# Split first weight loads, regrouped statistics and key rope sums in a two-layer trunk kernel

## The chip, the cores and the metric

The kernel runs on one core of one Trainium2 chip. The metric is the device time of one execution in microseconds (us); several executions are timed and their median is given. A profile of one execution shows each instruction of the five engines: TensorE (PE in the profile, its weight loads PEld), VectorE (DVE), ScalarE (ACT), GpSimd (POOL) and SyncE (SP), which here issues most DMA transfers.

## The reference

Two layers work on 528 tokens (16 meta tokens and 512 of the sequence) with 1024 channels in float32. Per layer:

```python
h = rmsnorm(x)
u_pool, z_pool, c_q, c_kv, k_rope, z_mla, g_pool, g_mla = split(h @ w_in)
y_pool = (pool_mix(u_pool) * silu(z_pool)) @ pool_w_up      # causal means over 2, 4, 8, 16 tokens
y_mla  = (mla(c_q, c_kv, k_rope) * silu(z_mla)) @ mla_w_up  # latent attention, 8 heads
x = x + (sigmoid(g_pool) * y_pool + sigmoid(g_mla) * y_mla) @ w_out
```

In `mla`, `c_q` (768 wide) and `c_kv` (256 wide) are RMS-normalised over their own width and expanded to queries, keys and values. A key head is 64 channels from `c_kv` and 32 channels of `k_rope`, which all heads share. Keys and queries are RMS-normalised per head (96 channels), the 32 channels get a rotary embedding, and attention is causal.

## The kernel before, in words

**Layout.** Channels lie on the 128 partitions, tokens along the free dimension. An activation tile is 128 channels by 528 tokens, and a matmul takes half of them, 264 (`HALF`). The first norm is not applied ahead of the products: they use x times the gain, and the token's factor `inv` is multiplied in where a product leaves PSUM.

**Products in three parts.** Weights and activations are split into a high and a low part, each of a type that TensorE multiplies faster than float32. ScalarE makes the high part, VectorE the low part by a subtraction. `mm3` (L184 to L186) is the three matmuls high·high, low·high and high·low. `split_h` (L336, L338) splits an input tile into `hh` and `hl`; `wload` (L179, L180) splits a weight chunk of 128 × 512 into `whi` and `wlo`.

**One stream of products.** `plan` lists all GEMMs in order: ckv0, ckv1, cq0 to cq4, then u0, k0, u1, kr, k1, u2, k2, u3, k3, the values v, and so on. `stream` goes through their weight chunks, with loads three to four ahead: `fetch` (L114) is a DMA on SP's queue into one of three `raw` buffers. `step` emits the next few matmuls of the stream; `upto(name)` emits until that GEMM is done, and `fill_now(ns)` emits matmuls for about so much time. Everything else is written between these calls, so it stands between matmuls of the stream in the program. A scheduler then orders the instructions on each engine; `behind(a, b)` forbids it to put a ahead of b. PSUM has four banks "mm", three "S" and one "o".

**Start.** ScalarE's queue loads the first 512 columns (four blocks of 128, one for each of the first four input tiles) of ckv0's weights (L121). SP's queue loads the gains `gn` (L122), input tile 0 (L123), the same columns of ckv1's weights, input tile 1, then the other input tiles (`other_loads`). TensorE multiplies ones (L136) meanwhile.

**Norm sums.** `norm_sums` adds squares over channels with a matmul by ones (L389). In layer 0 the sums over x come from ScalarE, which squares and adds rows of x (`row_sums`, L363), while matmuls of the stream are emitted; the sums over `c_kv` come from the squares that ScalarE makes of the product (L447). The sums go through DRAM (`nsr`), VectorE computes inverse roots, these go to DRAM (`ndr`), and two DMAs broadcast them to all partitions (`inv`, `cinv`; L427). `RET` is the time that is filled with products meanwhile.

**Key rope part.** `kr_body` (L455) has 32 columns of weights only, so four groups of 32 columns of the array work side by side on four input tiles, in float32; ScalarE copies the result and VectorE adds the four groups (L468, three adds for each half of the tokens). Later (`rest`, after `LAG`) it is multiplied by `inv`, copied to a second place by POOL, squared, scaled and rotated (`rope`).

**Statistics.** `stat` collects squared tiles, and `stat_go` (L496) sums them per head with a matmul whose weights are 8 columns wide. Each of the two token halves has two column groups, so four run side by side. It is called twice a layer, with 5 members (keys, `k_sums`) and with 7 (queries). `k_factors` reads the keys' sums back from DRAM (`ka`, L518), computes inverse roots and spreads them.

Of the kernel before, what the change touches and what calls it, by code (L numbers as in the profile page):

```python
# [9 lines left out]
F32 = mybir.dt.float32  # L10
# [8 lines left out]
P = 128  # L19
# [52 lines left out]
def trunk(ctx, tc, xT, xrow, mrow, pos, win, wkr, wqb, wkb, wvb, wgr, wpu, wmu, wout, gains, const, yT):  # L72
# [49 lines left out]
    first = sp.dma_start(gn, gains)  # L122
# [36 lines left out]
    vt = cp.tile([P, 4, H, P], F32R, name="vt")  # L159

    class Gemm:
        def __init__(self, name, src, width, evac=None, xs=None, segs=None, body=None, gain=None):
            self.name, self.src, self.width, self.alloc = name, src, width, mmt
            self.evac, self.xs, self.segs, self.body, self.gain = evac, xs, segs, body, gain
            self.spare = False

    loads = [0]

    def wload(src, n, gain, spare):
# [3 lines left out]
        if gain is not None:  # L173
            v = raw[:, :n].rearrange("p (k m) -> p k m", k=8)
            gp.tensor_mul(v, v, gain.unsqueeze(2).to_broadcast([P, 8, n // 8]))
            return raw, None
        hi = pool.tile([P, W if pool is tp else 512], F32R, tag=th, name=nm("whi"), bufs=nb)
        lo = pool.tile([P, W if pool is tp else 512], F32R, tag=tl, name=nm("wlo"), bufs=nb)
        act.activation(hi[:, :n], raw[:, :n], AF.Copy)  # L179
# [12 lines left out]
    def stream():  # L192
        flat = [(g_, c) for g_ in plan for c in range(0, g_.width, 512)]
        flat[1], flat[2] = flat[2], flat[1]

        def load(i):
            g_, c = flat[i]
            n = min(512, g_.width - c)
            return wload(g_.src[:, c:c + n], n, g_.gain, g_.spare)

        ahead = []
        for i in range(4):
            ahead.append(load(i))
            yield 0.0
        for i, (g_, c) in enumerate(flat):
            w = ahead.pop(0)
            if i >= 3 and i + 1 < len(flat):
                ahead.append(load(i + 1))
            final = c + 512 >= g_.width
            if g_.body is not None:  # L210
                yield from g_.body(c // 512, w)
# [101 lines left out]
    class Layer:  # L313
# [34 lines left out]

        def row_sums(self):
            sx = sm.tile([P, 2, 5], F32, tag="sx", name=nm("sx"))  # L350
            tags = ("q4", "q5", "q6", "q7", "kn0", "kn1", "kn2", "kn3", "kp")
            rows = []
            for i in range(2 * len(tags) + 4):
                step()
                if i % 2 == 0 and len(rows) < len(tags):
                    k = len(rows)
                    r, src = (P, xrow[:, k]) if k < 8 else (2 * NM, mrow)
                    rows.append(slot(tags[k])[0:r, 0:512])
                    behind(sp.dma_start(rows[k], src), newest[0])
                if i % 2 == 1 and i >= 5:  # L360
                    k = (i - 5) // 2
                    t = rows[k]
                    made = act.activation(t, t, AF.Square, accum_out=sx[0:t.shape[0], k % 2, k // 2:k // 2 + 1])  # L363
                    behind(made, newest[0])
                yield
            raw = nsr[0]
            sp.dma_start(raw[0:2, NM:T].rearrange("h (p i) -> p h i", i=4), sx[:, :, 0:4])
            sp.dma_start(raw[0:2, 0:NM].rearrange("h m -> m h"), sx[0:2 * NM, 0, 4:5])

        def norm_sums(self):  # L370
# [14 lines left out]
            for k in range(0, len(runs), 2):  # L385
                for s, (a, b) in enumerate(FULL):
                    for ps, t, m, start, stop in runs[k:k + 2]:
# [34 lines left out]
            fill_now(RET / 2)  # L422
            if self.l == 0:
                tables()
            fill_now(RET / 2)
            for i, d in enumerate((self.inv, self.cinv)):
                behind(sp.dma_start(d[:, 0:T], norms[i:i + 1, :].partition_broadcast(P)), newest[0])  # L427
            self.st = [sct(), sct()]
# [18 lines left out]
                self.csq_last = act.activation(self.csq[m][:, a:b], ps, AF.Square)  # L447
            return ev

        def kr_body(self, _, w):  # L450
            for a, b in FULL:
                ps = mmt()
                for k in range(8):
                    g = 32 * (k % 4)
                    pe.matmul(ps[g:g + 32, :b - a], w[0][:, 32 * k:32 * k + 32], self.xt[k][:, a:b],  # L455
                              start=k < 4, stop=k >= 4, tile_position=(0, g))
                self.ev_kr(ps[:, :b - a], a, b)
                yield 9 * (b - a) / 2.4

        def ev_kr(self, ps, a, b):  # L460
            n = b - a
            if a == 0:
                self.kraw = slot("kn3")
                self.kp = slot("kp")
            t = tmp()
            act.activation(t[:, :n], ps, AF.Copy)
            for g in (32, 64, 96):
                dve.tensor_add(t[0:32, :n], ps[g:g + 32, :], t[0:32, :n])  # L468

            def rest():  # L470
                dve.tensor_mul(t[:, :n], t[:, :n], self.inv[:, a:b])
                gp.tensor_copy(t[64:96, :n], t[0:32, :n])
                q = sqt()
                made = act.activation(q[:, :n], t[:, :n], AF.Square)
                self.stat(q[:, :n], a, b, C_KPE, made)
                kr = self.kraw[:, a:b]
                act.activation(kr, t[:, :n], AF.Copy, scale=self.g(G_KR))
                self.rope(self.kp[:, a:b], kr, a, b)
# [9 lines left out]
        def stat_go(self, members):  # L488
# [3 lines left out]
            for k, (s, a, b, q, c, made) in enumerate(batch):  # L492
                n = count[s]
                count[s] += 1
                g = 32 * s + 64 * (n % 2)
                mm = pe.matmul(self.st[s][g:g + H, a:b], cst[:, c:c + H], q, start=n < 2, stop=n >= members - 2,  # L496
                               tile_position=(0, g))
                if k < len(batch) - 1:
                    behind(mm, batch[-1][5])

        def stat_rows(self, x0):
# [450 lines left out]
        def register(self, nxt):  # L952
# [65 lines left out]
        def go(self, nxt):  # L1018
            l = self.l
            up = lambda name: upto((l, name))  # L1020
            if l == 0:
                for k in range(8):
                    if k in (0, 1, 3, 5):
# [133 lines left out]
```

## Time and profile before

| | us |
|---|---|
| median of 3 runs | 781.39 (781.0 to 783.37) |
| the profiled execution | 781.23 |
| its span, first to last instruction | 779.4 |
| TensorE busy | 773.5 (99% of the span) |
| VectorE, ScalarE, GpSimd busy | 537.7, 414.7, 206.8 |

A line of a timeline gives the start in us from the span's start, the duration, engine, line of the kernel, operation, output and inputs, shape and count; in brackets stands how long the engine was idle ahead of it and who ended that. A line of a grouped view gives the count, busy time in us and the mean of one in ns, and after a bar the idle time ahead. A line of a table by stretches gives the stretch, its length, the busy time of PE, PEld, DVE, ACT and POOL with counts, the granted clock, the busy share of the DMA engines and what they moved in GB/s. Matmuls are pipelined: the distance between starts tells what one costs.

### The profile page before, as it was taken

Reading aid. Unit: us, or ns where it says so; the run is one execution under the profiler, and the core shown is the slowest. Engines: PE = TensorE matmul, PEld = TensorE weight load, DVE = VectorE, ACT = ScalarE, POOL = GpSimd, SP = SyncE. Lnnn points to the kernel's source line nnn. Section 1 sums busy time; section 2 is a strip of 40 time slices with the busy share of each in tenths; the row PEclk is TensorE's granted clock in tenths of the full one; section 3 lists DMA queues with packets and bytes.
Section 4 is the critical chain, followed back from the end, with each engine's and each line's share of the span. In section 5 each row is a group of like instructions: output and inputs, shape, how many; then the busy total and the mean of one; then the engine's idle time right before and its main releaser. Section 6 shows DMA issues by size and latency. Waiting matters only on the chain.

```text
span 779.4 us, 14500 instructions
## 1 busy us (share of the span) xinstructions
PE 773.5 (99%) x5235; PEld 702.8 (90%) x5235; DVE 537.7 (69%) x1155; ACT 414.7 (53%) x930; POOL 206.8 (27%) x265
## 2 busy tenths in 40 slices
PE   8999999999999999999999999999999999999998
PEld 8999899999999999999998898887788888888887
DVE  5588687357788977685465577774477888755932
ACT  6755655545565665643354355455445666654420
POOL 1034504012334242053120235130132433420500
PEclk9999999999999999999999999999999999999999
DMA  8533233433322212234643322434242332222372
GB/s 281 163 112 89 83 123 99 116 87 101 92 88 86 82 55 81 80 97 147 186 135 97 103 82 90 132 88 142 69 129 89 96 86 81 66 81 68 105 240 88
DMA packets 54931, 84.04 MB, mean 108 GB/s; under 512 B 10006, under 2 KB 18582, under 8 KB 54860
## 3 DMA queue, kind: packets, MB, share of 16 engines
q1 hardware_dynamic: 54716, 82.86, 35.1%
q8 instruction: 41, 0.67, 0.4%
q14 instruction: 30, 0.25, 0.1%
q10 hardware_dynamic: 144, 0.26, 0.1%
HBM read 76.68 MB, written 4.29 MB: 104 GB/s over the span
## 4 chain that ended last, share of the span: by engine, by line
PE 97%; DMA 1%; DVE 1%; ACT 1%; issue 0%; SPq 0%; ACTq 0%
PE mm L184 29%; PE mm L186 28%; PE mm L185 28%; PE mm L838 2%; PE S L185 2%; PE S L186 2%; PE S L184 2%; PE o L843 1%; PE o L844 1%; PE S L496 1%; DMA raw<-win 1%; PE mm L455 0%; PE mm L867 0%; DMA ka<-ksr 0%; PE mm L389 0%
## 5 line engine op out<-in xcount | busy, mean ns | idle before, releaser
L184 PE MATMUL mm<-hh,whi 128*128 128x264 f32 (+2 forms) x1096 | 345.7, 317 | 1.0 <-DVE ky L289 0.5
L185 PE MATMUL mm<-hl,whi 128*128 128x264 f32 (+2 forms) x1096 | 343.1, 314 | 0.0
L186 PE MATMUL mm<-hh,wlo 128*128 128x264 f32 (+2 forms) x1096 | 342.6, 315 | 0.0
L180 DVE TENSOR_TENSOR wlo<-raw,whi 128x512 fp32r<-128x512 f32 (+2 forms) x251 | 186.6, 747 | 105.5 <-ACT whi L179 101.0
L179 ACT ACTIVATE whi<-raw 128x512 fp32r<-128x512 f32 (+2 forms) x251 | 150.8, 604 | 173.8 <-PE mm L185 131.3
L184 PEld LDWEIGHTS mm<-hh,whi 128*128 128x128 f32 x1096 | 205.6, 188 | 14.7 <-issue 1.6
L185 PEld LDWEIGHTS mm<-hl,whi 128*128 128x128 f32 x1096 | 206.1, 188 | 12.0
L186 PEld LDWEIGHTS mm<-hh,wlo 128*128 128x128 f32 x1096 | 205.3, 188 | 12.2
L742 POOL TENSOR_TENSOR tmp<-kp,bc 64x528 f32<-64x528 f32 x16 | 24.6, 1538 | 104.3 <-issue 89.0
L817 POOL TENSOR_TENSOR pm<-pa,rs 128x16 f32<-128x16 f32 x32 | 11.7, 366 | 148.5 <-DVE rs L812 148.5
L603 POOL TENSOR_TENSOR racc<-racc,tmp 128x264 f32<-128x264 f32 (+1 forms) x15 | 14.5, 969 | 120.6 <-ACT tmp L602 96.8
L927 POOL TENSOR_TENSOR tmp<-tmp,xb 128x264 f32<-128x264 f32 (+1 forms) x24 | 26.7, 1134 | 57.6 <-DVE tmp L925 55.4
L773 DVE CUSTOM_DVE_ANT_0 S<-S,maskw,nqs 128x272 f32<-128x272 f32 (+4 forms) x80 | 38.4, 498 | 2.3 <-PE S L186 1.9
L184 PE MATMUL mm<-u,whi 128*128 128x264 f32 (+1 forms) x108 | 35.2, 326 | 0.0
L186 PE MATMUL mm<-u,wlo 128*128 128x264 f32 (+1 forms) x108 | 34.7, 321 | 0.0
L184 PE MATMUL mm<-cq,whi 128*128 128x264 f32 (+1 forms) x108 | 34.7, 321 | 0.0
L186 PE MATMUL mm<-cq,wlo 128*128 128x264 f32 (+1 forms) x108 | 34.5, 321 | 0.0
L185 PE MATMUL mm<-cq,whi 128*128 128x264 f32 (+1 forms) x108 | 34.5, 321 | 0.0
L780 ACT ACTIVATE cq<-S,bia 128x400 f32<-128x400 f32 (+2 forms) x48 | 24.6, 516 | 18.5 <-DVE bia L807 9.4
L276 DVE TENSOR_TENSOR tl<-mm,th 128x512 fp32r<-128x512 f32 (+1 forms) x64 | 29.3, 483 | 6.7 <-ACT th L275 5.9
L819 POOL TENSOR_TENSOR cq<-cq,rs 128x384 f32<-128x384 f32 (+1 forms) x32 | 33.0, 1032 | 0.0
L275 ACT ACTIVATE th<-mm 128x512 fp32r<-128x512 f32 (+1 forms) x64 | 25.4, 434 | 6.2 <-PE mm L838 5.5
(271 smaller groups left out, 1372.4 us busy)
## 6 DMA issues: line engine op xcount, KB each, us to landing
raw<-win SPq DMA_DIRECT2D x143, 256.0 KB, 2.6
raw<-wout SPq DMA_DIRECT2D x32, 256.0 KB, 2.9
bc<-kdr SPq DMA_DIRECT2D x16, 264.0 KB, 3.4
raw<-wpu SPq DMA_DIRECT2D x16, 256.0 KB, 2.8
raw<-wmu SPq DMA_DIRECT2D x16, 256.0 KB, 2.6
raw<-wqb SPq DMA_DIRECT2D x12, 256.0 KB, 2.9
xb<-xT SPq DMA_DIRECT2D x8, 264.0 KB, 5.5
tmp<-xT SPq DMA_DIRECT2D x16, 132.0 KB, 2.9
```

What stands on the lines that cost most here:

```text
L179: act.activation(hi[:, :n], raw[:, :n], AF.Copy)
L180: dve.tensor_sub(lo[:, :n], raw[:, :n], hi[:, :n].bitcast(F32))
L184: pe.matmul(out, wh, xh, start=start, stop=False)
L185: pe.matmul(out, wh, xl, start=False, stop=False)
L186: newest[0] = pe.matmul(out, wl, xh, start=False, stop=stop)
L275: act.activation(hi[:, a:b], src, AF.Copy)
L276: dve.tensor_sub(lo[:, a:b], src, hi[:, a:b].bitcast(F32))
L742: gp.tensor_mul(kf[r0:r0 + 64, :], self.kp[r0:r0 + 64, :], bc[r0:r0 + 64, :])]
L773: dve.tensor_tensor_reduce(out=sv, in0=sv, in1=mask, scale=nqs[:, i, h:h + 1], scalar=3e38, op0=ALU.add, op1=ALU.min, accum_out=bia[:, c:c ...
L780: act.activation(pv, sv, AF.Exp, scale=-1.0, bias=bia[:, i:i + 1], accum_out=rs[:, c:c + 1])
L819: gp.tensor_mul(pt[i][:, NM:], pt[i][:, NM:], rs[:, i:i + 1].to_broadcast([P, n - NM]))
L927: gp.tensor_add(t[:, :b - a], t[:, :b - a], self.am[m][:, a:b])
```

## The change

- The first two weight chunks are loaded in two pieces. The first 128 columns of both (64 KB each) are issued on ScalarE's queue; the other 384 columns follow input tiles 0 and 1 on SP's queue. Each piece has its own cast and subtraction, those of the rests behind the cast of input tile 1.
- In layer 0 the norm sums are emitted after nine and not six pieces of `row_sums`, so 12 matmuls of cq1 stand ahead of them.
- The matmuls for the key rope part leave the stream. They stand directly behind the norm sums, in "S" banks, with their weights loaded by `kr_load` into a buffer of their own. Their copies and adds move there as well; what needs `inv` (`kr_rest`) comes after u1. Two row tiles of layer 0 use other buffers for that.
- In layer 0 `RET / 4` takes the place of the second `RET / 2` ahead of the two broadcasts.
- In `stat_go` the last, odd member of each half is cut into two halves of 132 tokens, one on each of its two column groups.
- `k_factors` and the second `columns` come after `up("cq5")`.

```diff
-    early.append(slot("rinv"))
-    act.dma_start(early[0][:, 0:512], win[0, MT_CKV, :, 0:512])
+    early += [slot("rinv"), rawt()]
+    for m in range(2):
+        act.dma_start(early[m][:, 0:P], win[0, MT_CKV + m, :, 0:P])
     first = sp.dma_start(gn, gains)
-    sp.dma_start(xb[:, 0, :T], xT[:, 0, :])
-    early.append(fetch(win[0, MT_CKV + 1, :, 0:512], 512, rawt(), sp))
-    sp.dma_start(xb[:, 1, :T], xT[:, 1, :])
+    for k in range(2):
+        sp.dma_start(xb[:, k, :T], xT[:, k, :])
+    for m in range(2):
+        sp.dma_start(early[m][:, P:512], win[0, MT_CKV + m, :, P:512])
...
-        act.activation(hi[:, :n], raw[:, :n], AF.Copy)
-        dve.tensor_sub(lo[:, :n], raw[:, :n], hi[:, :n].bitcast(F32))
+        head = P if loads[0] <= 2 else n
+        split(hi, lo, raw[:, 0:head], 0, head)
+        if head < n:
+            def rest(made):
+                behind(act.activation(hi[:, head:n], raw[:, head:n], AF.Copy), made)
+                dve.tensor_sub(lo[:, head:n], raw[:, head:n], hi[:, head:n].bitcast(F32))
+
+            rests.append(rest)
...
-            tags = ("q4", "q5", "q6", "q7", "kn0", "kn1", "kn2", "kn3", "kp")
+            tags = ("q4", "q5", "q6", "q7", "kn0", "kn1", "kn2", "bc", "bc")
...
+                if i == 0:
+                    self.kr_load()
...
-                for _ in range(6):
+                for _ in range(9):
                     next(rows)
...
+            self.kr_sums()
             sums = tmp()
...
-            fill_now(RET / 2)
+            fill_now(RET / 2 if self.l else RET / 4)
...
+        def kr_load(self):
+            self.wk = slot("kn3")
+            behind(sp.dma_start(self.wk[:, 0:256], wkr[self.l]), newest[0])
+            v = self.wk[:, 0:256].rearrange("p (k m) -> p k m", k=8)
+            g = gn[:, self.l * N_GAIN + G_H:self.l * N_GAIN + G_H + 8]
+            gp.tensor_mul(v, v, g.unsqueeze(2).to_broadcast([P, 8, 32]))
+
+        def kr_sums(self):
+            self.kp = slot("kp")
             for a, b in FULL:
-                ps = mmt()
+                ps = sct()
                 for k in range(8):
                     g = 32 * (k % 4)
-                    pe.matmul(ps[g:g + 32, :b - a], w[0][:, 32 * k:32 * k + 32], self.xt[k][:, a:b],
-                              start=k < 4, stop=k >= 4, tile_position=(0, g))
+                    mm = pe.matmul(ps[g:g + 32, :b - a], self.wk[:, 32 * k:32 * k + 32], self.xt[k][:, a:b],
+                                   start=k < 4, stop=k >= 4, tile_position=(0, g))
+                    behind(mm, self.csq_last)
+                t = self.kp[:, a:b]
+                act.activation(t, ps[:, :b - a], AF.Copy)
+                for g in (32, 64, 96):
+                    dve.tensor_add(t[0:32, :], ps[g:g + 32, :b - a], t[0:32, :])
+
+        def kr_rest(self, a, b):
             if a == 0:
                 self.kraw = slot("kn3")
-            def rest():
-                dve.tensor_mul(t[:, :n], t[:, :n], self.inv[:, a:b])
-                gp.tensor_copy(t[64:96, :n], t[0:32, :n])
...
-            after(LAG, rest)
+            t, kr = self.kp[:, a:b], self.kraw[:, a:b]
+            behind(dve.tensor_mul(t, t, self.inv[:, a:b]), newest[0])
+            gp.tensor_copy(t[64:96, :], t[0:32, :])
...
-                mm = pe.matmul(self.st[s][g:g + H, a:b], cst[:, c:c + H], q, start=n < 2, stop=n >= members - 2,
-                               tile_position=(0, g))
-                if k < len(batch) - 1:
+                cuts = [(a, b, g)] if n < members - 1 else [(a, HALF // 2, g), (HALF // 2, b, g + 64)]
+                for a0, b0, g in cuts:
+                    mm = pe.matmul(self.st[s][g:g + H, a0:b0], cst[:, c:c + H], q[:, a0 - a:b0 - a], start=n < 2,
+                                   stop=n == members - 1, tile_position=(0, g))
                     behind(mm, batch[-1][5])
...
-                if m == 1:
-                    add("kr", wkr[l], 256, body=self.kr_body, gain=gn[:, l * N_GAIN + G_H:l * N_GAIN + G_H + 8])
...
+                    if k == 1:
+                        for r in rests:
+                            r(self.made[1])
             if l:
+                self.kr_load()
                 up("ckv1")
             self.norm_sums()
             up("u1")
+            for a, b in FULL:
+                self.kr_rest(a, b)
+                fill_now(1300)
...
+            up("cq5")
             self.k_factors()
             self.eps = self.columns(2)
```

More of the change, by code (lines that the diff above doesn't have):

```diff
@@ L161, in trunk, with __init__, wload @@
     class Gemm:
-        def __init__(self, name, src, width, evac=None, xs=None, segs=None, body=None, gain=None):
+        def __init__(self, name, src, width, evac=None, xs=None, segs=None, body=None):
             self.name, self.src, self.width, self.alloc = name, src, width, mmt
-            self.evac, self.xs, self.segs, self.body, self.gain = evac, xs, segs, body, gain
+            self.evac, self.xs, self.segs, self.body = evac, xs, segs, body
             self.spare = False
     loads = [0]
-    def wload(src, n, gain, spare):
+    rests = []
+    def wload(src, n, spare):
         raw = early.pop(0) if early else fetch(src, n, rawt(), sp)
@@ L172, in wload @@
         pool, th, tl, nb = (tp, "th", "tl", 2) if loads[0] <= 2 or spare else (wp, "whi", "wlo", 3)
[L173 to L176, printed above, removed]
         hi = pool.tile([P, W if pool is tp else 512], F32R, tag=th, name=nm("whi"), bufs=nb)
         lo = pool.tile([P, W if pool is tp else 512], F32R, tag=tl, name=nm("wlo"), bufs=nb)
-        act.activation(hi[:, :n], raw[:, :n], AF.Copy)
-        dve.tensor_sub(lo[:, :n], raw[:, :n], hi[:, :n].bitcast(F32))
+        head = P if loads[0] <= 2 else n
[5 more added lines that the diff above has]
+            rests.append(rest)
         return hi, lo
@@ L198, in load @@
             n = min(512, g_.width - c)
-            return wload(g_.src[:, c:c + n], n, g_.gain, g_.spare)
+            return wload(g_.src[:, c:c + n], n, g_.spare)
         ahead = []
@@ L357, in row_sums @@
                     r, src = (P, xrow[:, k]) if k < 8 else (2 * NM, mrow)
-                    rows.append(slot(tags[k])[0:r, 0:512])
+                    rows.append(slot(tags[k], bufs=3 if tags[k] == "bc" else 1)[0:r, 0:512])
                     behind(sp.dma_start(rows[k], src), newest[0])
@@ L448, in ev_ckv @@
             return ev
-        def kr_body(self, _, w):
+        def kr_load(self):
[6 more added lines that the diff above has]
+            self.kp = slot("kp")
             for a, b in FULL:
-                ps = mmt()
+                ps = sct()
@@ L453, in kr_body @@
                 for k in range(8):
                     g = 32 * (k % 4)
-                    pe.matmul(ps[g:g + 32, :b - a], w[0][:, 32 * k:32 * k + 32], self.xt[k][:, a:b],
-                              start=k < 4, stop=k >= 4, tile_position=(0, g))
[L457 to L461, printed above, removed]
+                    mm = pe.matmul(ps[g:g + 32, :b - a], self.wk[:, 32 * k:32 * k + 32], self.xt[k][:, a:b],
+                                   start=k < 4, stop=k >= 4, tile_position=(0, g))
@@ L462, in ev_kr @@
+                    behind(mm, self.csq_last)
[4 more added lines that the diff above has]
+        def kr_rest(self, a, b):
             if a == 0:
                 self.kraw = slot("kn3")
[L464 to L468, printed above, removed]
@@ L470, in rest @@
-            def rest():
-                dve.tensor_mul(t[:, :n], t[:, :n], self.inv[:, a:b])
-                gp.tensor_copy(t[64:96, :n], t[0:32, :n])
[L473 to L478, printed above, removed]
-            after(LAG, rest)
+            t, kr = self.kp[:, a:b], self.kraw[:, a:b]
@@ L482, in stat @@
+            behind(dve.tensor_mul(t, t, self.inv[:, a:b]), newest[0])
+            gp.tensor_copy(t[64:96, :], t[0:32, :])
+            q = sqt()
+            made = act.activation(q[:, :b - a], t, AF.Square)
+            self.stat(q[:, :b - a], a, b, C_KPE, made)
+            act.activation(kr, t, AF.Copy, scale=self.g(G_KR))
+            self.rope(t, kr, a, b)
         def stat(self, q, a, b, c, made):
@@ L1022, in go @@
                 for k in range(8):
-                    if k in (0, 1, 3, 5):
+                    for _ in range((2, 0, 0, 1, 0, 1, 0, 0)[k]):
                         step()
```

## The prediction, made before the changed kernel had run

> **What bounds the kernel now.** I read the page's busy times and chain first, because they tell which engine has to get faster for the end to move.
>
> ```profile
> span 779.4 us, 14500 instructions
> PE 773.5 (99%) x5235; PEld 702.8 (90%) x5235; DVE 537.7 (69%) x1155; ACT 414.7 (53%) x930; POOL 206.8 (27%) x265
> PE 97%; DMA 1%; DVE 1%; ACT 1%; issue 0%; SPq 0%; ACTq 0%
> ```
>
> TensorE is busy for 773.5 of 779.4 us and is 97% of the chain. Nothing that only relieves another engine moves the end. Time can come from two places: the few gaps between TensorE's instructions, and TensorE work that is cut. So the next view is TensorE's timeline at the places that the change touches, the start first.
>
> ```profile
> 1.05 3.43 PE L136 MATMUL wps<-ones 128*128 128x128 f32 x16 [1.05 <-DVE na L718]
> 4.97 0.80 PE L184 MATMUL S<-hh,whi 128*128 128x264 f32 x2 [0.49 <-ACT hh L336]
> 6.45 0.39 PE L184 MATMUL mm<-hh,whi 128*128 128x264 f32 x1 [0.44 <-ACT whi L179]
> 7.53 0.41 PE L184 MATMUL S<-hh,whi 128*128 128x264 f32 x2
> 8.27 0.28 PE L186 MATMUL S<-hh,wlo 128*128 128x264 f32 x1
> ...
> 9.75 0.28 PE L186 MATMUL S<-hh,wlo 128*128 128x264 f32 x1
> 9.87 0.28 PE L184 MATMUL S<-hh,whi 128*128 128x264 f32 x1
> ```
>
> The warm-up ends at 4.48. The first product starts at 4.97, the second chunk's at 6.45; the row at 7.53 is the first with input tile 1, and from 8.27 matmuls follow each other every 0.12 us (9.75 to 9.87). The row at 9.87 is the first with tile 3. ScalarE, which makes the high parts, shows why:
>
> ```profile
> 3.65 0.63 ACT L179 ACTIVATE whi<-rinv 128x512 fp32r<-128x512 f32 x1 [0.98 <-DMA rinv<-win]
> 4.40 0.93 ACT L336 ACTIVATE hh<-xb,gn 128x264 fp32r<-128x264 f32 x2
> 5.77 0.63 ACT L179 ACTIVATE whi<-raw 128x512 fp32r<-128x512 f32 x1 [0.45 <-DMA raw<-win]
> 6.45 1.43 ACT L336 ACTIVATE hh<-xb,gn 128x528 fp32r<-128x528 f32 x2
> 8.52 0.74 ACT L336 ACTIVATE hh<-xb,gn 128x528 fp32r<-128x528 f32 x1 [0.65 <-DMA xb<-xT]
> ```
>
> It waits for transfers at 3.65 (first chunk), 5.77 (second chunk) and 8.52 (tile 3).
>
> **Start-up (estimate −0.55 us).** The change puts only 128 columns of each chunk, 64 KB of 256, ahead of tile 0, and the other 2 × 192 KB behind tile 1.
>
> ```profile
> 4.00:5.00 1.00, 0.51 (x5) 0.32 (x4) 0.69 (x2) 0.89 (x3) 0.00 (x0) 1.00 1.01 368
> xb<-xT SPq DMA_DIRECT2D x8, 264.0 KB, 5.5
> 0.74 0.39 SPq L122
> L179 ACT ACTIVATE whi<-raw 128x128 fp32r<-128x128 f32 x8 | 2.5, 306 | 0.8 <-PE mm L185 0.6
> ```
>
> The DMA engines are full (share 1.01) and move 368 GB/s. Through tile 0 the order was 256 + 24 (gains) + 264 = 544 KB; it becomes 128 + 24 + 264 = 416 KB, 0.35 us less. The head's cast costs 0.31 instead of 0.63. Tile 0's cast comes 0.35 to 0.6 earlier, so the first product starts near 4.45, just behind the warm-up. The second chunk's head is cast by 5.1 instead of 6.40, so both gaps before 6.45 go. Through tile 1 it is 680 KB; the second chunk in the old order ended at 800 KB and was there at 5.77, so tile 1 is there near 5.45. Its cast (0.74) ends near 6.2, the first rest's cast near 6.7: the first product with tile 1 starts near 6.75 instead of 7.53. What is late next is tile 3. All that lies ahead of it is the same 1,328 KB in both orders and it was waited for at 8.52, so its cast ends at 8.52 + 0.74 = 9.26 and TensorE can take it near 9.3 instead of 9.87. That is −0.55. Ends: if tile 3 comes 0.4 earlier, the density from tile 2 on (cast by about 7.9, ten spacings later) gives 8.95, −0.92; if transfers do not come earlier at all, 0. One more issue on SP's queue ahead of tile 2 and one on ScalarE's cost 0.4 each by the row of L122; the engines' backlog hides SP's, and ScalarE's lies before 3.65, in its 0.98 of idling. The two extra casts and subtractions lie in ScalarE's and VectorE's idle time before 8.52.
>
> Beside the row of 368 GB/s stands a rule against this edit: the Trainium skill, "DMA: Bandwidth & Descriptors", section "Bandwidth", gives a 64 KB load 0.95 us (138 GB/s) and calls smaller transfers descriptor-dominated. By that figure the two heads would take, as an estimate, 1.9 us and not 0.36, and the start would lose its gain. Here the queues already hold the next transfers, so I take the row.
>
> **The norm's column sums (−0.33 us).** They move 12 matmuls into the next GEMM.
>
> ```profile
> 23.63 0.28 PE L186 MATMUL mm<-hh,wlo 128*128 128x264 f32 x1
> 24.15 0.65 PE L389 MATMUL mm<-q,ones 128*32 128x264 f32 x8 [0.24 <-ACT q L447]
> 24.73 0.39 PE L184 MATMUL mm<-hh,whi 128*128 128x264 f32 x1
> 24.96 0.28 PE L185 MATMUL mm<-hl,whi 128*128 128x264 f32 x1
> ```
>
> From 23.63 to 24.96 lie 1.33 us for two ordinary spacings (0.24) and eight fp32 matmuls. To split the rest I need the price of such a batch without a wait. The key's rope batch shows it:
>
> ```profile
> 61.30 0.28 PE L186 MATMUL mm<-hh,wlo 128*128 128x264 f32 x1
> 61.51 1.99 PE L455 MATMUL mm<-xb,raw 128*32 128x264 f32 x32
> 63.42 0.39 PE L184 MATMUL mm<-kh,whi 128*128 128x264 f32 x1
> 63.65 0.28 PE L185 MATMUL mm<-kl,whi 128*128 128x264 f32 x1
> ```
>
> ```profile
> 61.75 0.63 PE L455 MATMUL mm<-xb,raw 128*32 128x264 f32 x8
> 62.87 0.63 PE L455 MATMUL mm<-xb,raw 128*32 128x264 f32 x8
> ```
>
> Four column groups start together; the second pass starts at 61.75, the seventh at 62.87, so a pass is 0.224, and eight are 1.79. From 61.30 to 63.65 are 2.35; less 0.24 and 1.79 this leaves 0.32 for entering and leaving such a batch. The column sums have two passes, 0.45, and 0.32: of their 1.33 − 0.24 = 1.09 the other 0.32 to 0.33 is the wait for the squares (ScalarE, L447). Twelve matmuls (1.45 us) cover it. Ends: −0.33, or 0 if the squares come later by as much.
>
> **Key rope sums behind the norm sums (−0.64 us).** The same 32 matmuls now follow the column sums directly, in both layers, so one entry and exit of 0.32 goes per layer. No row shows two batches joined; ends: 0, and −0.32 a layer. I take −0.32, since the second batch has the same shape of tile (128*32). The Trainium skill, "TensorEngine Tiling (Array Packing)", section "Tiling Modes", says that changing the tiling mode, not just the tile, drains TensorE; by it the drain between two equal batches falls away, and with a drain at each batch this term would be 0.
>
> What moves along: two ScalarE copies and six VectorE adds a layer, the weight load on SP (now in a slot of its own and not in the stream), the gain's multiply on POOL.
>
> ```profile
> 24.00:31.00 7.00, 6.85 (x59) 6.43 (x60) 3.80 (x7) 6.58 (x20) 0.76 (x1) 1.00 0.49 160
> L468 DVE TENSOR_TENSOR tmp<-mm,tmp 32x264 f32<-32x264 f32 x12 | 5.1, 428 | 0.4
> L466 ACT ACTIVATE tmp<-mm 128x264 f32<-128x264 f32 x4 | 1.5, 387 | 5.9 <-POOL tmp L562 5.7 <-DVE tmp L572 0.2
> ```
>
> VectorE is busy for 3.80 of 7 us there, so 6 × 0.43 = 2.57 fits. ScalarE is busy for 6.58, so its 2 × 0.39 = 0.77 makes what is queued behind it, the evacuations of the next GEMM and the weight casts, up to 0.77 later; the four "mm" banks and weight casts made a chunk ahead (24 matmuls of 0.12, 2.9 us) hide that. Without that cover it costs 0.77 in layer 0. The second halves, which multiply by the norm, come after u1, in stretches that lose the adds. RET/4 sends the broadcasts a quarter earlier, behind the write of the norms; the weight load behind them waits up to that write's landing, and u0's evacuation has less time to wait for. At TensorE: 0.
>
> **Statistics (−0.90 us).** In each of four calls the odd last member, which had half the column groups to itself, is cut into two halves on all four.
>
> ```profile
> 85.38 1.51 PE L496 MATMUL S<-sq,cst 128*8 128x264 f32 x20
> L496 PE MATMUL S<-sq,cst x88: 372/386/390, 85.4 to 544.3; 128*8 128x264 f32 x76, 128*8 128x248 f32 x12
> ```
>
> Five members on two groups each are three rounds of two passes (20 records), seven are four rounds. The last round's passes shrink from 264 to 132 columns: 2 × 0.112 = 0.224 a call, 0.90 in all. Ends: −0.90, and −0.45 if the short records are limited by their issue.
>
> **Key factors after cq5 (0).** The wait that this is next to:
>
> ```profile
> 91.79 0.18 DVE L518 TENSOR_SCALAR ka<-ka 128x33 f32<-128x33 f32 x1 [2.61 <-DMA ka<-ksr]
> 100.64 0.28 PE L186 MATMUL mm<-u,wlo 128*128 128x264 f32 x1
> 101.45 0.36 PE L184 MATMUL mm<-hh,whi 128*128 128x264 f32 x1 [0.53 <-DVE ky L289]
> ```
>
> VectorE stands for 2.61 us on a transfer and TensorE pays 0.81 − 0.12 = 0.69 nine microseconds later. In the changed kernel's order on VectorE ka stands between the same neighbours, so I leave the wait where it is.
>
> **Sum.** −0.55 − 0.33 − 0.64 − 0.90 = −2.42 us. The profiled execution took 781.23 (span 779.4 and 1.83 around it), 0.16 below the median of 781.39. 781.23 − 2.42 = 778.8.
>
> **The rivals.**
> 1. The start gains nothing, because the split pieces reach the chip no earlier and every transfer stays in one saturated queue order: −0.33 − 0.64 − 0.90 = −1.87, 779.4. For it: engines full from 2.5 us on, and tile 3 still decides. Against: fewer bytes ahead of tile 0. The 64 KB figure that was cited above from the Trainium skill, "DMA: Bandwidth & Descriptors", points to this case. Chance 0.2.
> 2. The wait at 100.64 goes too, if ka no longer stops VectorE for 2.61 us: −2.42 − 0.69 = −3.11, 778.1. Against: the order there is unchanged. Chance 0.1.
> 3. The moves do not do what they say: joined batches still pay both entries and the norm sums meet a new wait of the old size: −0.55 − 0.90 = −1.45, 779.8. For it: no row shows two batches joined. Against: equal shapes, and 1.45 us of cover. Chance 0.1.
> 4. Slower: the evacuations queue behind kr's adds and copies. VectorE runs in order, and the six adds wait for the end of the last key matmul; the residual casts (L180) and evacuations behind them come up to 2.57 + 0.77 = 3.34 us later in each layer. It decides once that exceeds the lead of the weight casts, 2.9 us, together with the rest of ScalarE's backlog; then TensorE loses most of 3.34 twice: −2.42 + 6.68 = +4.26, 785.5. For it: ScalarE at 6.58 of 7. Against: VectorE at 3.80 of 7, and layer 1, where ScalarE does not make the row sums. Chance 0.12.
>
> **How the numbers follow.** My forecast keeps 0.48: 778.8, its own range by the ends 778.0 to 780.2. About 0.3%, 2.34 us, is what a measurement of this kernel can tell from no change; that border is at 779.05, right beside the forecast. Faster: two thirds of 0.48, nearly all of case 2, and 0.15 of cases 1 and 3, when a term there is larger, 0.47 in all; slower is case 4, 0.12; the remainder, 0.41, is the same. The range leaves out case 4. It goes from 777.6 (all larger ends with case 2, −0.92 − 0.33 − 0.64 − 0.90 − 0.69 = −3.48, less the 0.16 between two executions) to 781.5, where cases 1 and 3 come together, half of the statistics' gain stays and ScalarE's 0.77 is not hidden (−0.45 + 0.77 = +0.32).
>
> **What would show it.** In the profile after: the first product near 4.45, the first with tile 3 near 9.3 and no later gap; no wait at L389's successor and the 32 kr records directly behind the column sums, with one entry; statistics calls of 24 and 32 records, each 0.22 shorter; the 0.69 near 99 unchanged. A TensorE wait on an evacuation near 27 to 33 us, on a weight cast behind the broadcasts near 47, or on VectorE's rope shuffle near 72 would make it wrong.

## The result: 0.16% slower, not 0.3% faster, and the profile after

The changed kernel takes 782.92 us in the median of 19 runs, the kernel before 781.94 in 19 runs beside it. The ratio is 1.0016, with a 95% interval of 1.0009 to 1.0022. The forecast was 778.8 and its range ended at 781.5. Of the 19 runs of the kernel before, six lie above 782.6 us, against 12 of 92 in the later sets, so its median here is 0.3 to 0.6 us higher than there (781.3 to 781.6). The profiled execution after took 782.78 us. The page's head, busy engines and chain:

```profile
span 780.7 us, 14541 instructions
PE 773.8 (99%) x5251; PEld 703.5 (90%) x5251; DVE 534.7 (68%) x1157; ACT 413.6 (53%) x932; POOL 205.8 (26%) x265
PE 94%; DVE 2%; DMA 1%; ACT 1%; issue 1%; SPq 0%; DVEq 0%; ACTq 0%
```

TensorE still bounds the kernel, but its share of the chain fell from 97% to 94% and VectorE's rose from 1% to 2%: there are new waits. The view of waits names them (who waited for whom, total, times, longest):

```profile
PE mm L189 <- DVE u L549: 1.2, 2, 1.0
...
PE mm L189 <- ACT whi L280: 0.5, 1, 0.5
PE mm L189 <- ACT whi L182: 0.4, 1, 0.4
PE S L189 <- ACT hh L341: 0.3, 1, 0.3
PE mm L189 <- DVE ky L294: 0.3, 1, 0.3
```

In the kernel before the wait for ky was 0.5 and the first two did not exist. TensorE's timeline after has them at three places beside the start: near 57, near 80 and near 473 us.

```profile
5.18 0.80 PE L189 MATMUL S<-hh,whi 128*128 128x264 f32 x2 [0.35 <-ACT hh L341]
...
8.13 0.39 PE L189 MATMUL mm<-hh,whi 128*128 128x264 f32 x1 [0.40 <-ACT whi L182]
...
10.25 0.28 PE L189 MATMUL S<-hh,whi 128*128 128x264 f32 x1
...
57.31 0.28 PE L191 MATMUL mm<-kh,wlo 128*128 128x264 f32 x1
58.10 0.36 PE L189 MATMUL mm<-hh,whi 128*128 128x264 f32 x1 [0.50 <-ACT whi L280]
...
80.01 0.28 PE L191 MATMUL mm<-kh,wlo 128*128 128x264 f32 x1
81.25 0.47 PE L189 MATMUL mm<-whi,kh 128*128 128x512 f32 x1 [0.95 <-DVE u L549]
```

The first product starts at 5.18 and not near 4.45, the first with tile 3 at 10.25 and not near 9.3; the wait of 0.40 at 8.13 is a new one, for the cast of the second rest (L182). Of 58.10 − 57.31 = 0.79 us 0.66 are wait, of 1.24 near 80 1.12; 0.33 follow at 82 and 0.40 at 473. What was foreseen for TensorE's own work did come:

```profile
25.48 0.28 PE L191 MATMUL mm<-hh,wlo 128*128 128x264 f32 x1
25.69 0.65 PE L396 MATMUL mm<-q,ones 128*32 128x264 f32 x8
26.16 1.96 PE L471 MATMUL S<-xb,kn 128*32 128x264 f32 x32
28.05 0.39 PE L189 MATMUL mm<-hh,whi 128*128 128x264 f32 x1
28.28 0.28 PE L190 MATMUL mm<-hl,whi 128*128 128x264 f32 x1
...
87.45 1.31 PE L507 MATMUL S<-sq,cst 128*8 128x264 f32 x24
...
102.50 0.28 PE L191 MATMUL mm<-u,wlo 128*128 128x264 f32 x1
103.06 0.37 PE L189 MATMUL mm<-hh,whi 128*128 128x264 f32 x1 [0.28 <-DVE ky L294]
```

The column sums follow their forerunner without a wait, and the key rope sums follow them without a second entry: 28.28 − 25.48 = 2.80 is 0.24 for two ordinary spacings, ten passes of 0.224, and 0.32 once. A statistics call takes 1.31 and not 1.51.

### The profile page after: what moved, and what is told of

Same layout as the page of the kernel before. It is cut to its first block, busy times and chain, and to the rows that moved or that the text cites. A ratio compares the mean times of both kernels' runs of the same rounds, so it can differ in the third digit from the quotient of the medians.

```text
span 780.7 us, 14541 instructions
## 1 busy us (share of the span) xinstructions
PE 773.8 (99%) x5251; PEld 703.5 (90%) x5251; DVE 534.7 (68%) x1157; ACT 413.6 (53%) x932; POOL 205.8 (26%) x265
## 4 chain that ended last, share of the span: by engine, by line
PE 94%; DVE 2%; DMA 1%; ACT 1%; issue 1%; SPq 0%; DVEq 0%; ACTq 0%
PE mm L189 28%; PE mm L191 27%; PE mm L190 27%; PE mm L848 2%; PE S L191 2%; PE S L190 2%; PE S L189 2%; PE o L853 1%; PE o L854 1%; PE S L507 1%; DVE wlo L281 1%; DMA raw<-win 1%; PE S L471 0%; DVE tmp L579 0%; PE mm L877 0%
## 5 line engine op out<-in xcount | busy, mean ns | idle before, releaser
L281 DVE TENSOR_TENSOR wlo<-raw,whi 128x512 fp32r<-128x512 f32 (+2 forms) x251 | 184.0, 736 | 107.8 <-ACT whi L280 103.8
L280 ACT ACTIVATE whi<-raw 128x512 fp32r<-128x512 f32 (+2 forms) x251 | 150.0, 601 | 176.4 <-PE mm L190 135.7
L280 ACT ACTIVATE th<-mm 128x512 fp32r<-128x512 f32 (+1 forms) x64 | 25.4, 434 | 6.5 <-PE mm L848 5.9
```

Of the source, the lines that this page charges most:

```text
L280: act.activation(hi[:, a:b], src, AF.Copy)
L281: dve.tensor_sub(lo[:, a:b], src, hi[:, a:b].bitcast(F32))
```

## The experiments

Theory A after this comparison: three separate losses, which are the short rows of the split load, the rotation (kr_rest) ahead of the pooling windows, and a late norm chain at 57 us. Each kernel below has five rounds beside the kernel before, which gave five runs of e5, six of e6, 12 of e8 and 11 of the others; for the changed kernel the 19 runs above stand. The table holds the ratio of each to the kernel before, and from its profile the start of the 61st product (when the steady flow has been reached) and the waits of TensorE, as gaps less the ordinary spacing. In the profiles of e5 and e11 the first products ran at half rate (last section), so their 61st product is late for that reason.

| kernel | ratio, 95% interval | 61st product | near 57 | near 80 | near 473 | near 100 |
|---|---|---|---|---|---|---|
| before | 1 | 13.50 | 0 | 0 | 0 | 0.69 |
| changed | 1.0016 (1.0009–1.0022) | 13.89 | 0.66 | 1.45 | 0.40 | 0.43 |
| e1 start-up alone | 1.0006 (0.9997–1.0015) | 13.48 | 0.82 | 0 | 0 | 0.67 |
| e2 statistics alone | 0.9992 (0.9983–1.0000) | 13.17 | 0.83 | 0 | 0 | 0.63 |
| e3 changed, old start-up | 1.0001 (0.9991–1.0011) | 12.99 | 0 | 1.43 | 0.40 | 0.54 |
| e4 changed, rotation late | 0.9995 (0.9986–1.0004) | 13.96 | 0.85 | 0 | 0 | 0.62 |
| e5 = e3 with rotation late | 0.9963 (0.9951–0.9976) | 15.21 | 0 | 0 | 0 | 0.45 |
| e6 = e5, tables early | 0.9970 (0.9959–0.9981) | 12.88 | 0 | 0 | 0 | 0.64 |
| e7 before, tables early | 0.9998 (0.9989–1.0007) | 13.03 | 0 | 0 | 0 | 0.63 |
| e8 before, 256-column heads | 1.0005 (0.9995–1.0014) | 13.07 | 0.54 | 0 | 0 | 0.67 |
| e9 = e3, rotation on VectorE | 0.9987 (0.9978–0.9996) | 13.35 | 0 | 0.87 | 0 | 0.99 |
| e10 = e5, members not cut | 0.9979 (0.9970–0.9988) | 13.34 | 0 | 0 | 0 | 0.69 |
| e11 = e4, tables early | 0.9990 (0.9981–0.9999) | 15.30 | 0 | 0 | 0 | 0.60 |

### e1, e3 and e8: the start-up

e1 is the kernel before with the loads, casts and steps of the new start-up; e3 the changed kernel without them.

> The kernel before with the start-up part of the change alone. Theory A: the 128-column pieces keep the DMA engines busy (0.89 to 0.98 from 2.0 to 3.5 us in the trace after) at 165 to 264 GB/s where the whole chunks moved 382 to 402, so tile 0 and the rests arrive later; the first product comes near 5.2, the steady flow is reached 0.3 us later than before, and the time is +0.3 us against before. Theory B (the prediction's step, with one unlucky set of transfers in the trace after): fewer bytes ahead of tile 0 pay, first product near 4.45, -0.55 us. A rival between them: tile 3 decides, 0.

> The changed kernel with the start-up of the kernel before. Theory A: 0.3 us faster than the changed kernel, about +0.7 us against before; the waits of TensorE near 57 (0.66), 80 (1.12), 82 (0.33) and 473 us (0.40) stay. Theory B: without the start-up's gain it is 0.55 us slower than the changed kernel, +1.5 us against before.

Measured: e1 782.06 us against 781.54, e3 781.27. The interval of e1 takes in no change, so its time alone does not decide; its first product starts at 5.39. By the ratios e3 is 0.15%, 1.2 us, below the changed kernel; the forecast had it 0.55 above. Two more pairs of the table differ by the start-up alone: e5 is 0.32%, 2.5 us, below e4, with intervals that do not touch, and e6 0.20%, 1.6 us, below e11. So the new start-up costs time. The transfers show where. Tables by stretches, the kernel before first, then the changed one (the last two columns are the DMA engines' busy share and the GB/s):

```profile
2.00:2.50 0.50, 0.50 (x5) 0.50 (x4) 0.00 (x0) 0.49 (x2) 0.46 (x2) 1.00 0.30 91
2.50:3.00 0.50, 0.50 (x4) 0.50 (x4) 0.00 (x0) 0.17 (x1) 0.46 (x2) 1.00 1.04 382
3.00:3.50 0.50, 0.50 (x4) 0.50 (x4) 0.00 (x0) 0.00 (x0) 0.49 (x1) 1.00 1.05 402
```

```profile
2.00:2.50 0.50, 0.50 (x5) 0.50 (x3) 0.00 (x0) 0.50 (x1) 0.46 (x2) 1.00 0.98 198
2.50:3.00 0.50, 0.50 (x4) 0.50 (x4) 0.00 (x0) 0.49 (x2) 0.46 (x2) 1.00 0.92 165
3.00:3.50 0.50, 0.50 (x4) 0.50 (x4) 0.10 (x1) 0.36 (x2) 0.49 (x1) 1.00 0.89 264
```

The engines are nearly as busy with the 128-column pieces as with whole chunks, at half the rate from 2.5 to 3.0. The transfers of each queue tell on what. A line gives packets, MB moved and the share of 16 engines' time; q10 is ScalarE's queue with the pieces, q1 SP's with the gains and input tile 0. The changed kernel from 2.0 to 2.5, then from 2.5 to 3.0:

```profile
q10 hardware_dynamic: 129, 0.06, 40.2%
...
q1 hardware_dynamic: 36, 0.08, 85.3%
q10 hardware_dynamic: 14, 0.01, 6.7%
```

The kernel before from 3.0 to 3.5, when tile 0 came in:

```profile
q1 hardware_dynamic: 72, 0.15, 76.7%
```

The pieces moved 0.06 MB in 40.2% of half a microsecond, which is about 300 GB/s. What was slow is tile 0, whose rows have 2112 bytes in both kernels: 0.08 MB in 85.3%, about 190 GB/s, where 0.15 MB in 76.7%, about 390, stood before. In e1 and e4 it was 0.05 MB in 81% to 82%. ScalarE waited 1.25 us for it and cast it at 4.62, where 4.40 stood:

```profile
4.62 0.92 ACT L341 ACTIVATE hh<-xb,gn 128x264 fp32r<-128x264 f32 x2 [1.25 <-DMA xb<-xT]
```

So the low rate is not that of the short rows. Why tile 0's own rows are slow when the pieces go ahead of them stays open. The next experiment was made to test the width of the rows (its edit against e1; the rests and the cast follow):

```diff
-        act.dma_start(early[m][:, 0:P], win[0, MT_CKV + m, :, 0:P])
+        act.dma_start(early[m][:, 0:2 * P], win[0, MT_CKV + m, :, 0:2 * P])
...
```

> The kernel before with the start-up split, the first piece 256 columns wide (rows of 1024 bytes) and not 128 (512 bytes). Theory A (short rows are moved slowly): from 2.0 to 3.5 us the rate is between the 165 to 264 GB/s of 128 columns and the 382 to 402 of whole chunks, the steady flow is reached between them, +0.25 us against before. Rival (two more transfers and casts cost, whatever their width): as with 128 columns, +0.5 us. Rival of the prediction (fewer bytes ahead of tile 0 pay once the rate is full): -0.3 us.

e8's table:

```profile
2.00:2.50 0.50, 0.50 (x5) 0.50 (x4) 0.00 (x0) 0.50 (x1) 0.46 (x2) 1.00 0.73 203
2.50:3.00 0.50, 0.50 (x4) 0.50 (x4) 0.00 (x0) 0.49 (x2) 0.46 (x2) 1.00 1.09 247
3.00:3.50 0.50, 0.50 (x4) 0.50 (x4) 0.00 (x0) 0.50 (x2) 0.48 (x1) 1.00 0.80 243
```

The rate lies between, with 247 where 165 and 382 stood, but here too it is lost on SP's queue (0.08 MB in 83.2% from 2.5 to 3.0, about 190 GB/s), so this does not show that the width of the pieces' rows sets it. The time, 782.01 against 781.61, cannot be told from no change. In the profiles the 61st product starts at 13.48 to 13.96 with the new start-up (changed, e1, e4) and at 12.88 to 13.50 with the old one (before, e2, e3, e6, e7, e9, e10), e5 and e11 left out: about 0.6 us lost in the mean. e8, at 13.07, lies among the old ones. The profile of before on which the prediction rests was the latest of its kind. The 0.6 and a wait of up to 0.85 near 57 us, treated below, do not make up the 2.5 us between e4 and e5; what the rest is stays open.

### e2 and e10: the statistics

> The kernel before with the cut of the last statistics member alone. Theory A: each of the four calls is 0.22 us shorter, -0.9 us. Rival: the short records are limited by their issue, -0.45 us; or, since TensorE gets earlier and a wait behind it stays where it is (the 0.69 near 100), the two calls for keys give nothing, also near -0.45.

> The kernel of e5 without the cut of the last statistics member: what is left of the change is the norm sums and the key rope sums behind them, with the rotation behind the windows. Theory A: the cut is worth 4 x 0.22 = 0.9 us, so this is 0.9 slower than e5 and -1.8 us against before; the 0.33 for the wait ahead of the norm sums and 0.32 for each joined batch make 1.0 of that, and the wait near 57 that does not come in these kernels the rest. Rival: the cut gives half, then -2.2 us against before.

e2 took 780.78 us against 781.54 (−0.08%, interval −0.17% to 0), which does not tell −0.9 from −0.45. Between e10 (779.98) and e5 (778.87), in two different sets of runs, lie 0.16% of the ratios, about 1.2 us. The call has 24 records in 1.31 us in e2 too. The full gain of 0.2 a call is what the profiles show.

### e4 and e5: the rotation behind the windows

```diff
-            for a, b in FULL:
-                self.kr_rest(a, b)
-                fill_now(1300)
             self.ninv = self.columns(1)
             for m in range(2):
                 self.mix(m, self.window(m))
+            for a, b in FULL:
+                self.kr_rest(a, b)
+                fill_now(1300)
```

> The changed kernel with kr_rest moved behind the two pooling windows and mixes that follow u1. Theory A: the rope's POOL and VectorE work ahead of the windows pushes the windows' adds and the mixes onto u2, k2 and u3, where they hold the evacuation of u3; with the order turned, the waits near 80, 82 and 473 go (1.9 us in all) and the one near 57 stays: about -0.9 us against before. Rival: those waits come from the norm's chain, which is 2.3 us later against TensorE than before, or from VectorE instructions being slow beside POOL in any order; then they stay or move, and the time is that of the changed kernel, +1.0 us against before.

> The changed kernel with both findings put right: start-up of the kernel before, and kr_rest behind the two pooling windows. Theory A (the parts add up): the split start-up costs 0.55 us (steady flow at 13.9, 13.5, 14.0 with it and 13.5, 13.2, 13.0 without), the rope ahead of the windows 2.1 us (1.7 near 80, 0.45 near 473): about 2 us faster than the changed kernel, -1.5 us against before. What can take it back: the wait of 0.7 to 0.9 us near 57, which came in four of the six traces, also where the code up to there is that of the kernel before; if the norm's chain through DRAM sets it, an earlier start is lost there and the gain is -0.8 us.

e4: 781.43 against 781.54, and no wait near 80, 82 or 473. e5: 778.87 against 781.61, ratio 0.9963. With the old start-up and the later rotation the other edits bring 0.37%, 2.9 us; this version beats both kernels. The later rotation alone brings 0.21%, 1.6 us, with the new start-up (changed and e4) and 0.38%, 3.0 us, with the old one (e3 and e5, which has only five runs), where the profiles count waits of 1.85 and 1.83. All that the view of waits still has for TensorE in e5, apart from the warm-up:

```profile
PE mm L181 <- DVE ky L286: 0.3, 1, 0.3
PE S L181 <- ACT hh L333: 0.2, 1, 0.2
```

e5's profiled execution took 780.99, two us over its median, because its first products ran at half rate (last section); the other columns of its row are not touched by that, except that TensorE came late to 57 us.

Why the order matters is seen on VectorE and POOL in the changed kernel, where the windows' adds (L572) fall on u3's end:

```profile
78.14 1.09 POOL L572 TENSOR_TENSOR tmp<-u 128x542 f32<-128x542 f32 x1 [1.93 <-DVE tmp L582]
79.31 1.41 POOL L572 TENSOR_TENSOR tmp<-tmp 128x540 f32<-128x540 f32 x1
```

```profile
77.98 0.17 DVE L582 TENSOR_TENSOR tmp<-tmp,cst 128x16 f32<-128x16 f32 x1
78.28 1.50 DVE L281 TENSOR_TENSOR wlo<-raw,whi 128x512 fp32r<-128x512 f32 x1
79.70 1.05 DVE L583 TENSOR_TENSOR tmp<-tmp,u 128x16 f32<-128x16 f32 x1
80.68 0.42 DVE L549 TENSOR_TENSOR u<-mm,rinv 128x264 f32<-128x264 f32 x1
```

A subtraction that takes 0.69 alone takes 1.50 beside POOL's add, and one on 16 columns 1.05 instead of 0.17; it ends when POOL's add ends. Behind them, in order, stands u3's evacuation, which frees the bank for the values: it starts at 80.68. The Trainium skill, "SBUF — State Buffer", section "Who interferes with whom", says that a VectorE instruction with two SBUF inputs and a POOL instruction that reads SBUF lock each other out for a whole instruction; these durations agree.

### e9: the rotation on VectorE

```diff
-            gp.tensor_copy(t[64:96, :], t[0:32, :])
+            dve.tensor_copy(t[64:96, :], t[0:32, :])
-            self.rope(t, kr, a, b)
+            self.rope(t, kr, a, b, dve)
```

Here `dve` is the engine for the last multiply and add of kr's rotation.

> The kernel of e3 (the changed kernel with the start-up of before) with the six POOL instructions of kr_rest in each layer, two copies and the multiplies and adds of the rotation, put on VectorE; the order in the program stays, kr_rest ahead of the windows. Theory A: POOL's queue is the cause, since the windows' adds stand behind 0.7 + 0.5 + 0.9 + 0.8 + 0.8 + 1.1 us of kr's work and run beside VectorE's later instructions; with POOL free the windows start at once, the waits near 79 to 81 (1.55 us in the profile of e3) and 471 (0.4) go, and the time is that of e5, -2.7 us against before. Rival: VectorE's own order is the cause (the rotation ahead of the mixes); the waits stay or grow with 12 more instructions on VectorE, 0 to +1 us against before.

780.55 against 781.50: 0.13% faster, between both expectations. The wait near 473 went, the one near 80 fell from 1.43 to 0.87, and the one near 100 grew to 0.99. So POOL's queue is part of the cause. The rest lies with VectorE's order: POOL was free, but the first window's add did not start at once, it waited for the last add of the rotation on VectorE:

```profile
71.40 1.09 POOL L564 TENSOR_TENSOR tmp<-u 128x542 f32<-128x542 f32 x1 [13.27 <-DVE kp L533]
```

Only moving the rotation removes both.

### e6, e7 and e11: the wait near 57

It came in the changed kernel, e1, e4 and e8, but also in e2, whose code is that of before up to 85 us. There u0's evacuation is late; only in the changed kernel's profile the wait is put down to a weight cast (L280), which ends 0.03 us behind it, at 57.98. Its forerunners on VectorE and ScalarE stand behind the sines of the position tables, these behind the inverse roots, and these behind the read of the norm sums from DRAM (L418 after, L410 in e3). The edit puts the tables ahead of that read:

```diff
+            if self.l == 0:
+                tables()
             fill_now(2600)
             nq = sm.tile([16, 4, C], F32, tag="nq", name=nm("nq"))
...
-            if self.l == 0:
-                tables()
```

> The kernel of e5 with the position tables (sine and cosine) computed ahead of the read of the norm sums, and not behind the inverse roots. Theory A: near 57 TensorE waits for u0's evacuation, whose forerunners stand behind ScalarE's table load and two sines, and these behind the norm sums' read from DRAM, which lands at 35.9 to 39.6 us; with the tables early this chain is broken, the wait of 0.7 to 0.9 is gone in the profile, and the time is 0.7 us below that of e5. Rival: the chain goes through the broadcast of the inverse root to u0's evacuation; then the wait stays and the time is that of e5.

> The kernel before with only the tables moved ahead of the read of the norm sums. Theory A: the wait near 57 belongs to the kernel before too, in some executions (its profile lacks it, two profiles with the same code up to there have 0.82 us): -0.4 us on the median, and no wait near 57 in the profile. Rival: it comes from the norms and not from the tables; 0, and a wait of up to 0.8 in the profile.

> The kernel of e4 (the changed kernel, its start-up too, with the rotation behind the windows) with the tables ahead of the read of the norm sums. The profile of e4 has the wait near 57 us (0.85). Theory A: the read of the norm sums lands late against TensorE (39.60 us, where e5, without the wait in time, has 39.34 with TensorE 1.1 us later), and the tables behind the inverse roots carry this to u0's evacuation through ScalarE; with the tables early no wait comes near 57 and the time is 0.85 us below e4's, about -1.2 us against before. Rival: the wait moves to where the tables now stand (e7 had 0.54 near 43), or the inverse roots themselves come late; then as e4, -0.4 us.

e6 took 779.32 against 781.61 and has no wait, but e5, without the edit, has none to lose; the expected 0.7 did not come. e7 is the same as before (ratio 0.9998): no wait near 57, but one of 0.54 near 43, where ScalarE now has the sines. e11 against e4 points the way expected (0.9990 and 0.9995), but the intervals overlap, and the profile has a late TensorE there, so it does not decide. What the traces show is the order of SP's writes and the read. Changed kernel, then e3:

```profile
31.76 0.39 SPq L374 DMA_DIRECT2D nsr<-sx  x1
...
32.77 0.63 SPq L375 DMA_DIRECT2D nsr<-sx  x1
36.46 0.34 SPq L418 DMA_DIRECT2D nq<-nsr  x1
```

```profile
28.57 0.61 SPq L367 DMA_DIRECT2D nsr<-sx  x1
31.57 0.39 SPq L366 DMA_DIRECT2D nsr<-sx  x1
...
34.45 0.33 SPq L410 DMA_DIRECT2D nq<-nsr  x1
```

In the changed kernel, e4 and e11 the scheduler puts the write for the meta tokens (0.63) last and not first; with the new start-up alone (e1, e8) it stays first. The read is issued 3.7 us behind it, at 36.46, 2.0 later than in e3, while TensorE is only 0.9 later. VectorE gets the sums at 39.11 and 36.51. This points to the start-up's change for this wait too: the four profiles with it that ran at full rate and had the tables in their old place (changed, e1, e4, e8) all have the wait, and of five with the old start-up (before, e2, e3, e9, e10) only e2. It is not settled, since e1 and e8 have the wait with the writes in the old order, and e2 has it with the old start-up. In e2 the sums reached VectorE 1.0 later than before (36.94 and 35.92), with the read issued 0.4 later (34.32 and 33.92) and TensorE 0.3 earlier; what delayed them stays open.

## Why the prediction was wrong, step by step

By stretches of the two profiles (starts of the same product in both), against the terms of the sum:

| step | forecast | profile |
|---|---|---|
| start-up | −0.55 | +0.39 |
| norm sums and joined key rope sums | −0.97 | −1.22 |
| statistics | −0.90 | −0.8 |
| key factors after cq5, the wait near 100 | 0 | −0.26 |
| kr_rest after u1 | 0 | +1.70 and +0.50 |
| u0's evacuation behind the broadcasts | 0 | +0.66 |

The rows add up to +0.97. The last product of the stream starts 1.40 later (777.38 and 775.98); the other 0.4 lies in small differences that the rows do not name.

**Start-up: the step failed.** The 0.35 us for 128 KB less was worked out with 368 GB/s, measured with whole chunks, as if the rate stayed. From 2.0 to 3.5 us the engines moved 437 KB before (91, 382 and 402 GB/s) and 313 KB after (198, 165 and 264). These 124 KB take back nearly all that was saved, and tile 0 was cast 0.2 later and not 0.35 to 0.6 earlier. The slow part was tile 0's own transfer. The rule cited against the edit (a 64 KB load at 138 GB/s, in the Trainium skill's "DMA: Bandwidth & Descriptors") was the better guide to the outcome, although that page took its figure with loads issued from GpSimd. It does not name the cause seen here: the pieces ran at about 300 GB/s while they moved. The queues did hold the next transfers, which was the reason for leaving the rule, but these were slow. The rival that let the start gain nothing was nearest, and even it set the loss at 0. The dense stretch does begin with tile 3 again, but its cast no longer waits for its own transfer. ScalarE's timeline after has it as the second of two, directly behind tile 2's, which waited for tile 2:

```profile
8.31 1.38 ACT L341 ACTIVATE hh<-xb,gn 128x528 fp32r<-128x528 f32 x2 [0.23 <-DMA xb<-xT]
```

It ends at 8.31 + 1.38 = 9.69, where 8.52 + 0.74 = 9.26 stood, and the first product with tile 3 starts 0.38 later (10.25 and 9.87).

**Norm sums, joined batches: right.** The wait of 0.33 went. One entry and exit a layer went, worth 0.44 to 0.45 by the stretches and not 0.32. **Statistics: right**, 0.2 a call.

**kr_rest after u1: the step that cost most.** The prediction said that what needs the norm lies "in stretches that lose the adds" and set 0. It counted VectorE's busy time, which indeed fell (537.7 to 534.7), and not the order. The rotation's six POOL instructions and its place on VectorE push the windows' adds and the mixes by up to 7 us onto u2, k2 and u3. The slower rival named a queue of evacuations, but at kr's adds near 27 us and for want of cover of 2.9 us; nothing waited there. The list of what would show the forecast wrong had a wait on VectorE's rope shuffle near 72; it came one step behind, on u3's evacuation at 80.

**u0's evacuation: the cover was thinner than said.** The profile of before had no wait at 57, so the 0.66 was put at nothing. The profile of e2 shows that the same code has it at times: TensorE and the norm's chain arrive almost together. In such an execution a start that is earlier by some tenths would be lost there; no run here shows that by itself.

**Key factors:** the order on VectorE did stay; the wait went from 0.69 to 0.43 in this profile, and lies between 0.43 and 0.99 in the others, so its change is not settled.

## What to carry to other kernels

Do not carry the rate of a whole load over to a split one: the transfer that follows the pieces can lose its rate, so read what each queue moved in a profile of the split form. When work leaves a dense place, follow each of its instructions to the queue where it lands and ask which instruction stands behind it there and whom that one releases: total busy time does not tell. Compare several profiles before a step of 0.5 us is put on one wait or its absence, since a chain through DRAM can be a microsecond earlier or later in the same code.

## What the runs showed of the hardware that was not expected

- With pieces of 128 columns, of 256 columns and with whole chunks ahead of tile 0 the DMA engines moved 165, 247 and 382 GB/s in the same half microsecond (2.5 to 3.0), 0.92 to 1.09 busy. The rate was lost on tile 0's rows of 2112 bytes (about 190 GB/s, 390 before) and not on the 512-byte rows (about 300).
- A VectorE instruction on 128x16 took 1.05 us and not 0.17 while POOL added two SBUF tiles.
- In two of the 13 profiles (e5, e11) the first products ran at half rate to about 10.5 us, although the column of the granted clock says 1.00. TensorE in e5's profile, 0.22 from start to start and then 0.12:

```profile
9.97 0.42 PE L182 MATMUL S<-hl,whi 128*128 128x264 f32 x1
10.19 0.42 PE L183 MATMUL S<-hh,wlo 128*128 128x264 f32 x1
10.41 0.32 PE L181 MATMUL S<-hh,whi 128*128 128x264 f32 x1
10.57 0.28 PE L182 MATMUL mm<-hl,whi 128*128 128x264 f32 x1
10.69 0.28 PE L183 MATMUL mm<-hh,wlo 128*128 128x264 f32 x1
```

The 61st product then starts 2.2 us later (15.21 and 12.99 in e3). The Trainium skill, "TensorE: Matmul & The Clock Gate", part 1 on the clock gate, tells of half rate until a fixed window has been busy, with a point that varies by run; the spacing agrees, the column does not show it.
